# One 128-row tile for the first factors of both heads in a chunked delta-rule kernel

## The chip, the cores and the metric

The kernel runs on one core of a Trainium2 chip. The metric is the device time of one execution in microseconds (us); three runs of the kernel before took 2252.33, 2254.09 and 2258.38 us, so its median is 2254.09 us. The engines are called as the profile calls them: PE is the tensor engine's matmul and PEld its weight load, DVE the vector engine, ACT the scalar engine, POOL the GpSimd engine, SP the engine that issues most of the DMAs.

## What is computed

One layer of a hybrid decoder trunk over 1024 new tokens and 8 sequences of 8 decoded tokens, in float32. An input projection feeds three token mixers, whose gated outputs go through an output projection. The change concerns the first mixer, RWKV-7 with 16 heads of 64 features. Cut to what matters here, its reference is:

```python
def wkv7_scan(r, w, k, v, kk, a, s0):
    def step(S, inp):
        r_t, w_t, k_t, v_t, kk_t, a_t = inp
        sa = jnp.einsum('bhij,bhj->bhi', S, -kk_t)
        S = (S * w_t[:, :, None, :] + sa[..., None] * (kk_t * a_t)[:, :, None, :]
             + v_t[..., None] * k_t[:, :, None, :])
        return S, jnp.einsum('bhij,bhj->bhi', S, r_t)
```

The kernel takes 64 tokens (a chunk) at a time. Within a chunk it needs four products of every head, each a sum over the head's 64 features: the two first factors of the state's update (kk·a and k, both divided by the running decay) against the two second factors (−kk and r, both multiplied by it). Masked to the past, one of them is the triangular matrix N that is then inverted, and the others correct the outputs.

## The kernel before, in words

**Blocks and ticks.** Tokens go in two blocks (b = 0 and 1) of 512; block 0 also carries the 64 decoded tokens. In each block the input projection runs column tile after column tile as dense products on PE (`dense`, lines 237, 240, 243: three products per step, into the PSUM tile `dps`), then the output projection (lines 1360 to 1362). Between two steps of the dense products stands a call of `tick()`. Everything else is written as Python generators that issue a few instructions, then yield a number of ticks to let pass. The table `Y[b][u]` gives that number for each of the 54 yields of a unit; it is the same in both kernels. So the order of the instructions on each engine is fixed by hand when the program is built, and each engine works through its own queue in order. The dense products are the background; a side instruction on PE that waits holds up the dense products behind it.

**Units.** `rwkv_unit` (line 562) handles one pair of heads p (8 pairs) for one half u of a block: 4 chunks, or 5 in block 0's second half, where the fifth chunk holds the decoded tokens. There are 32 units, 8 of them with a fifth chunk, so 136 chunks in all. Head 0 of the pair lies in rows (partitions) 0 to 63, head 1 in rows 64 to 127. In the code `r` is the rows of the head at hand and `e` those of the other head.

**Around the change.** A unit does, in this order:
- `BE` is a chunk's first factors. It has three slots of 64 columns: slot 1 is k over the decay for both heads at once (line 647, one DVE product on 128 rows), slots 0 and 2 are the other factor of head 0 and of head 1 (line 667, written by the helper `st` on line 558, on 64 rows each). Head h takes slots h and h + 1.
- `KG` is the second factors, two heads by two slots. A head's own rows are filled by POOL (line 664, and 666 for the fifth chunk) and by DVE (line 670, through line 558). The other head's rows are written later, by `gmask_k` (line 697).
- `gmm` (line 677) makes the within-chunk products into the PSUM tiles `gp`, one matmul per chunk and head, on the 64 rows of the head. The trace counts two matmul instructions for each of these float32 products, so two chunks of both heads are 8. A unit issues its four chunks in two groups of two; a fifth chunk goes ahead as a group of its own.
- `gmask_n`, `gmask_q`, `gmask_k` read `gp` on DVE. N goes to DRAM and back for the inversion on POOL (lines 779, 780).
- `xv` is transposed into `vp` (line 732) and copied to `SV` (line 751).
- `BE` is transposed on PE, one 64-row transposition per chunk and head, into two PSUM tiles `bp` (line 758), and copied by ACT into the block-diagonal operand `Q2` (line 761).
- `bo` (line 769) sums the bonus, and so on; then the chunk recurrence runs `cp`, `W`, `cu`, `cq` (lines 871 to 895) chunk after chunk, each step a PE product, a DVE and an ACT copy.

The PSUM tiles `gp`, `vp`, `bp`, `bo`, `cq`, `fp` and others come from one pool of four buffers (`ps_s`) which they take in turn: the fifth request waits until the first is read out. Two units are under way at a time, so the recurrence of one lies between the preparations of the next on every engine.

Of the kernel before, what the change touches and what calls it, by code (L numbers as in the profile page):

```python
# [18 lines left out]
P = 128  # L19
# [35 lines left out]
def tile_trunk(  # L55
# [24 lines left out]

    # ---------------------------------------------------------------- constants
    ident = ctile([P, P], "ident")
# [24 lines left out]

    # ---------------------------------------------------------------- normalised inputs
    # the operand of a block's products, high and low parts, four feature tiles each
    act2 = [actp.tile([P, 4, 2, BLK + ND], F32R, name=f"a{j}") for j in range(4)]  # L110
# [32 lines left out]

    # ---------------------------------------------------------------- dense pieces
    wcount = [0]
# [18 lines left out]
    def out_plan(b):  # L164
        # column group, feature tile, token tiles
        if b == 1:
            return [(g, k, range(4)) for g in range(4) for k in range(NK)]
        return [(g, k, range(5)) for g in range(3) for k in range(NK)] + [(3, k, t) for t in (range(2), range(2, 5)) for k in range(NK)]
# [8 lines left out]
    class Feed:  # L177
        # the weights' pieces in their order: loads run ahead of the splits, and those ahead of the products
        def __init__(self):
# [33 lines left out]

    # generators that go on beside the products, in ticks of those
    pending, slot, seq = [], [0], [0]
# [32 lines left out]
    def dense(b, ct, hi, lo, feed, part=None):  # L248
        # part: the first half, where it is there already
        assert feed.src[feed.i] == (ct, 0)  # L250
        spans = ((0, UN), (UN, BLK + ND)) if b == 0 else ((0, BLK),)
        ps = [part or psd_tile()] + [psd_tile() for _ in spans[1:]]
        todo = list(zip(spans, ps))[1 if part else 0:]
        steps = 0
        for kh in range(4):
            piece = feed.piece(LS)
            for (t0, t1), q in todo:
                for k in range(4 * kh, 4 * kh + 4):
                    dense_k(q, hi, lo, k, piece, t0, t1, b == 1)
                    steps += 1  # L260
                    if steps < NK * len(todo):
                        tick()
                    if steps % len(todo) == 0:
                        feed.ahead(steps // len(todo) % 4)
        if b == 0:
            return [ps[0][:, :UN], ps[1][:, :UN + ND]]
        return [ps[0][:, :UN], ps[0][:, UN:]]
# [4 lines left out]
    with tc.tile_pool(name="prep", bufs=2) as pp, tc.tile_pool(name="setup", bufs=1) as sp, tc.manual_schedule():  # L272
        # the gain's row, spread over the partitions by the tensor engine
        grow = sp.tile([1, DM], F32, name="grow")
# [85 lines left out]
        def rescale(tt):  # L360
            # the scale of a tile as a diagonal, which its transposition multiplies by
            d = pp.tile([P, P], F32, name=f"dg{tt}", bufs=1)
# [175 lines left out]

    # ---------------------------------------------------------------- RWKV branch
    def shift_evac(wk, b, ct, ps, xs, u):  # L540
        # token shift of half a column tile: (1 - mu) * now + mu * before
        mu = pcol[:, MU + ct:MU + ct + 1]
# [19 lines left out]
    def rwkv_unit(wk, b, p, u, lora, lw, got, pair_ops, zk):  # L562
        # yields the steps of the dense products to let pass before it goes on
        dec = b == 0 and u == 1
# [27 lines left out]

        # decay, in-context rate, squared key norms
        sq, sqh = tmp("sq"), tmpr("sqh")
# [46 lines left out]

        BE = wk.tile([P, nch, 3, 64], F32, tag="BE", name="BE")
        yield Y[b][u][5]
        dve.tensor_mul(kp[:, :n], kp[:, :n], xk[:, :n])  # L644
        recip(0)
        yield Y[b][u][6]
        dve.tensor_mul(BE[:, :, 1, :], c3(kp), c3(Di))
        recip(1)
# [10 lines left out]
        yield Y[b][u][10]  # L659
        # phase operands of a chunk and head, in the rows of the head: keys and queries;  # L660
        # in the other head's rows: their products with the chunk's keys
        KG = wk.tile([P, nch, 2, 2, 64], F32, tag=f"KG{u}", name="KG")
        for h, r, _ in hs:
            pool_e.tensor_tensor(KG[r, 0:4, h, 1 - h, :], pair(xr)[r], Dp[r, :, 1:65], op=ALU.mult)
            if dec:
                pool_e.tensor_tensor(KG[r, 4, h, 1 - h, :].rearrange("p (b t) -> p b t", t=8), decv(xr)[r], Dd[r, :, 1:9], op=ALU.mult)
            st(BE[r, :, 2 * h, :], c3(xk)[r], dcol(HKK)[r], c3(Di)[r])
            yield Y[b][u][11]
        for h, r, _ in hs:
# [3 lines left out]
            yield Y[b][u][12]  # L673
        # within-chunk products, masked to the past
        N = wk.tile([P, nch, 64], F32, tag=f"N{u}", name="N")

        def gmm(gps, cs):
            for c in cs:
                for h, r, _ in hs:
                    pe.matmul(gps[h][:, c % 4 * P:(c % 4 + 1) * P], lhsT=BE[r, c, h:h + 2, :].rearrange("p a s -> p (a s)"),  # L680
                              rhs=KG[r, c, h].rearrange("p a s -> p (a s)"), start=True, stop=True)

# [16 lines left out]

        # X = (I - N)^-1: diagonal blocks of 16 by substitution, then blocks of 32 and 64  # L700
        ndr = drb.tile([5, 2, XS], F32, tag="ndr", name="ndr")
# [43 lines left out]
        sync.dma_start(Xu[:U], units(ndr))  # L745
        # per head: the states, then the corrections, in the rows of the head, and the values in the others
        SV = wk.tile([P, nch, 2, 64], F32, tag=f"SV{u}", name="SV")
# [6 lines left out]
        yield Y[b][u][20]  # L754
        bps = [ps_s("bp") for _ in range(2)]
        for c in range(nch):
            for h, r, _ in hs:
                pe.transpose(bps[h][:, c * 64:(c + 1) * 64], BE[r, c, h:h + 2, :].rearrange("p a s -> p (a s)"), ident[r, r])
        yield Y[b][u][21]
        for h in range(2):  # L760
            act_e.copy(Q2[:, :nch, h, h, :], c3(bps[h]))
            if not h:
                yield Y[b][u][22]
        if dec:
# [11 lines left out]
        for r in range(1, 15):  # L776
# [4 lines left out]
            if dec and r == 7:  # L781
                # states of the decoded sequences
                zp = ps_s("zp")
# [70 lines left out]
        act_e.copy(XB[64:96, :nch, 1, 32:64], d3[64:96])  # L854
        # chunk recurrence
        yc = wk.tile([P, UN + ND], F32, tag="yc", name="yc")
# [5 lines left out]

        # chunks one after the other; the decoded rows beside the first
        for c in range(4):
# [38 lines left out]
            for i, q in enumerate(cs):  # L903
                for h, _, e in hs:
                    dve.tensor_tensor(yc[e, q * 64:(q + 1) * 64], yc[e, q * 64:(q + 1) * 64], cz[i][e, h], op=ALU.add)
        # group norm (token-major), bonus and gate (feature-major)
        sm = wk.tile([P, 8], F32, tag="sm", name="sm")
# [65 lines left out]

    # ---------------------------------------------------------------- pooling branch
    NU_ = 15 + UN + NB * 23
# [32 lines left out]

    # ---------------------------------------------------------------- in-projection of a block
    def in_block(wk, b, hi, lo, feed, part, raws):  # L1010
# [28 lines left out]
        def start(ps):  # L1039
            for u in range(2):  # L1040
# [10 lines left out]
                yield 1  # L1051
            # stationary operands of both heads of a pair; the blocks between the heads stay zero
            for u in range(2):
# [65 lines left out]
        pool_group(1)  # L1119
        # spatial gating  # L1120
        vn = [wk.tile([P, 2, 512], F32, tag=f"KG{u}", name=f"vn{u}") for u in range(2)]
# [72 lines left out]
        def states():  # L1194
            # states that leave
            if b == 0:
# [47 lines left out]

    # ---------------------------------------------------------------- out-projection of a block
    def cat_load(b, k):
# [9 lines left out]
    def first_cats(b, hi, lo, raws):  # L1256
        # the first rows of the out-projection, as soon as the last column tile has read what they overwrite
        yield D[7]
# [9 lines left out]
    def out_block(op, b, hi, lo, feed, raws):  # L1268
# [12 lines left out]
        if b == 0:  # L1281
            # the decoded rows: high and low parts side by side, so that two passes carry all their products
            dk = op.tile([P, NK, 2, ND], F32R, name="dk")
# [36 lines left out]
        def next_rows(j):  # L1320
            # a quarter of the next block's normalised inputs, feature-major
            for tt in range(4):
# [41 lines left out]
        def close(g, tt, q):  # L1364
# [10 lines left out]
            if g < 3:  # L1375
# [3 lines left out]
                return  # L1379
            # the norm of a row's end  # L1380
            _, dst, rr = rows[tt]
# [27 lines left out]

        # the tiles of a group begin and end one after the other  # L1410
        lags = ((0, 0, 1, 1, 3), (0, 0, 1, 2))[b]
# [72 lines left out]
```

## Time and profile before

| what | value |
|---|---|
| median of three runs | 2254.09 us (2252.33 to 2258.38) |
| span of the profiled execution | 2252.0 us |
| within-chunk products (line 680), PE instructions | 544, of 64 rows by 128 columns, 128 moving columns |
| transpositions of `BE` (line 758), PE instructions | 272, of 64 rows by 128 columns, 64 moving columns |
| copies of `bp` into `Q2` (line 761) on ACT | 64 |
| `BE` slot 1 (line 647) on DVE | 32 |

The profile is one execution on the chip with the start and end of every instruction. The ends of matmuls are modelled, so time on PE is best read from start to start. A row of the view in order of time gives the start, the time taken, the engine, the line, the operation, what it writes and reads, for PE the rows and columns of the tile (`64*128` is 64 rows by 128 columns), the shape and the number of instructions merged; in brackets the time that the engine was idle before it and who ended that. A row of the view of waits gives who waited for whom, the sum in us, the number of times, and the longest.

### The profile page before, as it was taken

Reading aid. Unit: us, or ns where it says so; the run is one execution under the profiler, and the core shown is the slowest. Engines: PE = TensorE matmul, PEld = TensorE weight load, DVE = VectorE, ACT = ScalarE, POOL = GpSimd, SP = SyncE. Lnnn points to the kernel's source line nnn. Section 1 sums busy time; section 2 is a strip of 40 time slices with the busy share of each in tenths; the row PEclk is TensorE's granted clock in tenths of the full one; section 3 lists DMA queues with packets and bytes.
Section 4 is the critical chain, followed back from the end, with each engine's and each line's share of the span. In section 5 each row is a group of like instructions: output and inputs, shape, how many; then the busy total and the mean of one; then the engine's idle time right before and its main releaser. Section 6 shows DMA issues by size and latency. Waiting matters only on the chain. (4 is left out here: it accounts for less than half of the span.)

```text
span 2252.0 us, 40898 instructions
## 1 busy us (share of the span) xinstructions
PE 2163.5 (96%) x14706; PEld 1860.5 (83%) x14706; DVE 1212.4 (54%) x2978; ACT 1006.0 (45%) x2680; POOL 1066.7 (47%) x1820
## 2 busy tenths in 40 slices
PE   7999999999999999999999999999999999999998
PEld 6998988988889899998887777777777778887786
DVE  6477677567667523214236467767676753323313
ACT  5344554554555442223334445555556454222323
POOL 5455555554555534223335455655555463432332
PEclk9999999999999999999999999999999999999999
DMA  5232232322222233336545432222222233334634
GB/s 153 77 75 64 75 78 58 76 72 65 74 70 70 74 87 96 93 95 195 175 150 178 129 81 77 74 72 77 75 73 78 72 85 95 95 116 129 191 122 140
DMA packets 390306, 221.18 MB, mean 98 GB/s; under 512 B 124054, under 2 KB 355736, under 8 KB 389207
## 3 DMA queue, kind: packets, MB, share of 16 engines
q1 hardware_dynamic: 390104, 218.58, 34.0%
q8 instruction: 116, 1.90, 0.4%
q14 instruction: 86, 0.70, 0.1%
HBM read 191.90 MB, written 26.61 MB: 97 GB/s over the span
## 5 line engine op out<-in xcount | busy, mean ns | idle before, releaser
L237 PE MATMUL dps<-a,whi 128*128 128x256 f32 (+1 forms) x2544 | 883.6, 347 | 2.1 <-ACT whi L154 1.9
L243 PE MATMUL dps<-a,wlo 128*128 128x256 f32 (+1 forms) x2544 | 844.5, 332 | 1.1 <-POOL wlo L161 0.7
L240 PE MATMUL dps<-a,whi 128*128 128x256 f32 (+1 forms) x2544 | 843.0, 331 | 0.0
L161 POOL TENSOR_TENSOR wlo<-raw,whi 128x512 fp32r<-128x512 f32 x415 | 550.5, 1330 | 591.2 <-ACT whi L154 541.7
L237 PEld LDWEIGHTS dps<-a,whi 128*128 128x128 f32 x2544 | 484.7, 191 | 48.9 <-issue 10.2
L243 PEld LDWEIGHTS dps<-a,wlo 128*128 128x128 f32 x2544 | 484.1, 190 | 33.5 <-POOL wlo L161 1.1
L240 PEld LDWEIGHTS dps<-a,whi 128*128 128x128 f32 x2544 | 485.5, 191 | 26.0 <-issue 0.2
L154 ACT CAST whi<-raw 128x512 fp32r<-128x512 f32 x552 | 338.6, 620 | 351.9 <-PE dps L240 117.4
L161 DVE TENSOR_TENSOR wlo<-raw,whi 128x512 fp32r<-128x512 f32 x137 | 101.8, 743 | 164.3 <-ACT whi L154 163.7
L1360 PE MATMUL ops<-whi,a 128*128 128x512 f32 x448 | 176.6, 394 | 2.5 <-ACT a L1253 1.8
L1361 PE MATMUL ops<-wlo,a 128*128 128x512 f32 x448 | 176.8, 395 | 2.2 <-POOL wlo L161 1.7
L1362 PE MATMUL ops<-whi,a 128*128 128x512 f32 x448 | 175.1, 391 | 0.1
L779 POOL TENSOR_TENSOR Tu<-Xu,Nu 32x14 f32<-32x14 f32 (+9 forms) x448 | 127.0, 283 | 27.3
L780 POOL TENSOR_TENSOR Xu<-Xu,Tu 32x14 f32<-32x14 f32 (+9 forms) x448 | 120.6, 269 | 35.1
L1361 PEld LDWEIGHTS ops<-wlo,a 128*128 128x128 f32 x448 | 84.1, 188 | 23.8 <-POOL wlo L161 5.6
L1360 PEld LDWEIGHTS ops<-whi,a 128*128 128x128 f32 x448 | 84.1, 188 | 22.0 <-ACT a L1253 2.3
L898 ACT ACTIVATE ZD<-SV,DC 64x64 f32<-64x64 f32 x192 | 66.2, 345 | 79.9 <-DVE SV L558 77.2
L1362 PEld LDWEIGHTS ops<-whi,a 128*128 128x128 f32 x448 | 84.1, 188 | 19.5 <-DVE a L1254 1.8
L922 POOL TENSOR_TENSOR sv<-sv,neghalf 128x4 f32<-128x4 f32 (+1 forms) x32 | 37.1, 1158 | 132.8 <-DVE sv L921 116.5
L871 PEld LDWEIGHTS cp<-SV,KG 128*128 128x128 f32 x544 | 77.5, 190 | 24.6 <-DVE SV L558 19.8
L871 PE MATMUL cp<-SV,KG 128*128 128x64 f32 x544 | 81.4, 271 | 9.6 <-DVE SV L558 9.6
L892 PEld LDWEIGHTS cq<-SV,Q 128*128 128x128 f32 x544 | 76.4, 190 | 15.3 <-DVE SV L885 11.0
(318 smaller groups left out, 3103.2 us busy)
## 6 DMA issues: line engine op xcount, KB each, us to landing
raw<-in_w_in_dram SPq DMA_DIRECT2D x424, 256.0 KB
raw<-in_w_out_dram SPq DMA_DIRECT2D x144, 256.0 KB
raw<-cat SPq DMA_DIRECT2D x32, 256.0 KB
res<-in_x_prompt_dram SPq DMA_DIRECT2D x32, 256.0 KB
out_dram<-res SPq DMA_DIRECT2D x32, 256.0 KB
x<-in_x_prompt_dram SPq DMA_DIRECT2D x4, 1024.0 KB
x<-in_x_prompt_dram SPq DMA_DIRECT2D x6, 512.0 KB
ndr<-N SPq DMA_DIRECT2D x48, 64.0 KB
```

The lines of the kernel that those rows point to most:

```text
L154: act_e.copy(whi, raw[:, :512])
L161: eng.tensor_sub(wlo, raw[:, :512], whi.bitcast(F32))
L237: pe.matmul(o, lhsT=wh, rhs=xh, start=(k == 0), stop=False)
L240: pe.matmul(o, lhsT=wh, rhs=xl, start=False, stop=False)
L243: pe.matmul(o, lhsT=wl, rhs=xh, start=False, stop=(k == NK - 1))
L779: pool_e.tensor_tensor(tv, bc(Xu[:U, 0:r, r], 2, e), bc(Nu[:U, r, r + 1:16], 1, r), op=ALU.mult)
L780: pool_e.tensor_tensor(Xu[:U, 0:r, r + 1:16], Xu[:U, 0:r, r + 1:16], tv, op=ALU.add)
L871: pe.matmul(cw[i][:, h], lhsT=KG[:, q, h].rearrange("p a t -> p (a t)"), rhs=SV[:, q, h, :], start=True, stop=True)
L892: pe.matmul(cz[i][:, h], lhsT=Q2[:, q, h].rearrange("p a t -> p (a t)"), rhs=SV[:, q, h, :], start=True, stop=True)
L1360: pe.matmul(q, lhsT=ah, rhs=whi, start=(k == 0), stop=False)
L1361: pe.matmul(q, lhsT=ah, rhs=wlo, start=False, stop=False)
L1362: pe.matmul(q, lhsT=al, rhs=whi, start=False, stop=(k == NK - 1))
```

## The change

`BE` gets two slots in place of three: slot h holds the kk·a factor of head h in the rows of head h, and slot 1 − h the k factor in the same rows. The 128 columns of a chunk are then a single stationary operand for both heads. To fill it, the product of line 647 is made twice, on 64 rows each, since the heads' columns now differ. The second factors `KG` are set to zero in the other head's rows by two POOL memsets ahead of the products of lines 664 and 666, and `gmm` multiplies all 128 rows of `BE` by all 128 rows of `KG`; the zeros keep the heads apart. The transposition is one per chunk, of 128 rows, and fills one PSUM tile for four chunks (two in the units with a fifth chunk). One ACT copy moves both heads of up to four chunks into `Q2`.

```diff
-        BE = wk.tile([P, nch, 3, 64], F32, tag="BE", name="BE")
+        BE = wk.tile([P, nch, 2, 64], F32, tag="BE", name="BE")
...
-        dve.tensor_mul(BE[:, :, 1, :], c3(kp), c3(Di))
+        for h, r, _ in hs:
+            dve.tensor_mul(BE[r, :, 1 - h, :], c3(kp)[r], c3(Di)[r])
...
         KG = wk.tile([P, nch, 2, 2, 64], F32, tag=f"KG{u}", name="KG")
+        for h, _, e in hs:
+            pool_e.memset(KG[e, :, h], 0.0)
         for h, r, _ in hs:
...
-            st(BE[r, :, 2 * h, :], c3(xk)[r], dcol(HKK)[r], c3(Di)[r])
+            st(BE[r, :, h, :], c3(xk)[r], dcol(HKK)[r], c3(Di)[r])
...
-                for h, r, _ in hs:
-                    pe.matmul(gps[h][:, c % 4 * P:(c % 4 + 1) * P], lhsT=BE[r, c, h:h + 2, :].rearrange("p a s -> p (a s)"),
-                              rhs=KG[r, c, h].rearrange("p a s -> p (a s)"), start=True, stop=True)
+                for h in range(2):
+                    pe.matmul(gps[h][:, c % 4 * P:(c % 4 + 1) * P], lhsT=BE[:, c].rearrange("p a s -> p (a s)"),
+                              rhs=KG[:, c, h].rearrange("p a s -> p (a s)"), start=True, stop=True)
...
-        bps = [ps_s("bp") for _ in range(2)]
+        bps = [ps_s("bp") for _ in range(1 + dec)]
         for c in range(nch):
-            for h, r, _ in hs:
-                pe.transpose(bps[h][:, c * 64:(c + 1) * 64], BE[r, c, h:h + 2, :].rearrange("p a s -> p (a s)"), ident[r, r])
+            pe.transpose(bps[c // 4][:, c % 4 * P:(c % 4 + 1) * P], BE[:, c].rearrange("p a s -> p (a s)"), ident)
         yield Y[b][u][21]
-        for h in range(2):
-            act_e.copy(Q2[:, :nch, h, h, :], c3(bps[h]))
-            if not h:
-                yield Y[b][u][22]
+        for i, bp in enumerate(bps):
+            m = min(nch - 4 * i, 4)
+            act_e.copy(Q2[:, 4 * i:4 * i + m].rearrange("p c h k j -> p c (h k) j")[:, :, 0::3, :],
+                       bp[:, :m * P].rearrange("p (c h j) -> p c h j", h=2, j=64))
+        yield Y[b][u][22]
```

The lines below this are five further down in the kernel after. What moves on three engines, in the queues as the programs are built:

On DVE, a unit of block 1 before, from the first product of k to the second reciprocal (`sq` is the squared key norm, `W` the copy of the other unit's recurrence):

```order
L644 TENSOR_TENSOR kp<-kp,xk 128x256
L640 RECIPROCAL sq<-sq 128x64
L905 TENSOR_TENSOR yc<-yc,cq 64x64 x2
L875 COPY W<-cp 64x64
L647 TENSOR_TENSOR BE<-kp,Di 128x4x64
L640 RECIPROCAL sq<-sq 128x64
```

and the same place of the kernel after:

```order
L645 TENSOR_TENSOR kp<-kp,xk 128x256
L640 RECIPROCAL sq<-sq 128x64
L910 TENSOR_TENSOR yc<-yc,cq 64x64 x2
L880 COPY W<-cp 64x64
L649 TENSOR_TENSOR BE<-kp,Di 64x4x64 x2
L640 RECIPROCAL sq<-sq 128x64
```

One instruction of 128 rows has become two of 64 rows; nothing else on DVE changes its place.

On POOL, a unit of block 1 before, around the second factors (`wlo` is the low part of a piece of weights for the dense products, `kpl` a low part for `bo`):

```order
L780 TENSOR_TENSOR Xu<-Xu,Tu 32x14
L161 TENSOR_TENSOR wlo<-raw,whi 128x512 x2
L664 TENSOR_TENSOR KG<-xr,D 64x4x64 x2
L161 TENSOR_TENSOR wlo<-raw,whi 128x512
L719 TENSOR_TENSOR kpl<-kp,kph 128x256
```

and after:

```order
L785 TENSOR_TENSOR Xu<-Xu,Tu 32x14
L161 TENSOR_TENSOR wlo<-raw,whi 128x512 x2
L666 MEMSET KG 64x4x128 x2
L668 TENSOR_TENSOR KG<-xr,D 64x4x64 x2
L161 TENSOR_TENSOR wlo<-raw,whi 128x512
L723 TENSOR_TENSOR kpl<-kp,kph 128x256
```

Two memsets stand ahead of the products, behind whatever wait for the old `KG` those had.

On PE, a unit of block 1 before, around the transpositions of `BE`:

```order
L240 MATMUL dps<-a_111,whi 128x512
L243 MATMUL dps<-a_111,wlo 128x512
L758 MATMUL bp<-ident,BE 128x64 x8
L237 MATMUL dps<-a_111,whi 128x512
L240 MATMUL dps<-a_111,whi 128x512
```

and after:

```order
L240 MATMUL dps<-a_111,whi 128x512
L243 MATMUL dps<-a_111,wlo 128x512
L762 MATMUL bp<-ident,BE 128x128 x4
L237 MATMUL dps<-a_111,whi 128x512
L240 MATMUL dps<-a_111,whi 128x512
```

Eight transpositions of 64 rows are four of 128 rows, at the same place. The within-chunk products keep their number and their places.

## The prediction

> **What bounds the kernel now.** I read the page first, then the chain that ended last, then the waits, and then PE and DVE in order of time at the places of the change.
>
> ```profile
> span 2252.0 us, 40898 instructions
> ...
> PE 2163.5 (96%) x14706; PEld 1860.5 (83%) x14706; DVE 1212.4 (54%) x2978; ACT 1006.0 (45%) x2680; POOL 1066.7 (47%) x1820
> ...
> PE dps L243 6%; PE dps L237 6%; PE dps L240 6%; PE ops L1362 2%; PE ops L1361 2%; PE ops L1360 2%; DVE sq L640 1%; DMA raw<-in_w_out_dram 1%; DVE KG L558 1%; PE gp L680 1%; PE cq L892 1%; DVE BE L558 1%; DVE kp L558 1%; DVE kp L644 1%; DVE SV L558 1%
> ```
>
> PE is busy nearly throughout and DVE half of the time. Yet the last line, the chain by line, has DVE's preparation of `kp`, `sq`, `BE` and `KG` in it. The chain in order of time shows how it gets there (start, time, what), here in a unit of block 1:
>
> ```profile
> 1380.01 0.41 PE cq L892 x4
> 1380.44 0.28 DVE SV L558
> ...
> 1382.57 0.83 DVE BE L647
> ...
> 1389.40 0.48 DVE KG L558
> 1390.05 1.27 DVE KG L558
> 1391.45 0.68 PE gp L680 x6
> ```
>
> From 1380.4 to 1391.3 the chain stays on DVE: a queue without a gap, released by PE's `cq`, until the within-chunk products can go on. The waits confirm it, and hold two more rows that the change touches:
>
> ```profile
> PE gp L680 <- DVE KG L558: 13.8, 18, 3.0
> PE bp L758 <- ACT SV L751: 1.9, 7, 0.3
> PE bo L769 <- ACT yf L963: 1.2, 7, 0.2
> ```
>
> So at `gp` PE waits for DVE, and what makes DVE later there makes PE later by as much.
>
> **The change, PE's own work.** First the rows: a group of eight products behind no wait (block 1, a unit's second group), eight products of 128 rows of the same length (line 1181), eight transpositions of 64 rows and four of 128 rows (line 1128), each with the dense products around.
>
> ```profile
> 1393.30 0.40 PE L243 MATMUL dps<-a,wlo 128*128 128x512 f32 x1
> 1393.63 0.71 PE L680 MATMUL gp<-KG,BE 64*128 64x128 f32 x8
> 1394.27 0.50 PE L237 MATMUL dps<-a,whi 128*128 128x512 f32 x1
> ```
>
> ```profile
> 1994.70 0.39 PE L243 MATMUL dps<-a,wlo 128*128 128x512 f32 x1
> 1994.93 1.05 PE L1181 MATMUL mixp<-wsT,vn 128*128 128x128 f32 x8
> 1995.74 0.48 PE L237 MATMUL dps<-a,whi 128*128 128x512 f32 x1
> ```
>
> ```profile
> 1438.42 0.39 PE L243 MATMUL dps<-a,wlo 128*128 128x512 f32 x1
> 1438.74 0.46 PE L758 MATMUL bp<-ident,BE 64*128 64x64 f32 x8
> 1439.13 0.50 PE L237 MATMUL dps<-a,whi 128*128 128x512 f32 x1
> ```
>
> ```profile
> 1901.21 0.39 PE L243 MATMUL dps<-a,wlo 128*128 128x512 f32 x1
> 1901.44 0.60 PE L1128 MATMUL tp<-ident,vf 128*128 128x128 f32 x4
> 1901.80 0.47 PE L237 MATMUL dps<-a,whi 128*128 128x512 f32 x1
> ```
>
> *Products.* From dense start to dense start the 64-row group takes 1394.27 − 1393.30 = 0.97 us, the 128-row group 1.04. "All rows" therefore gains nothing: the two heads already share the array, and what 64-row tiles lose on the way in (the first starts 0.33 behind the dense product, where the 128-row one starts 0.23 behind) they win back by running beside each other. There are 40 such groups behind no wait (8 in block 0's first halves, 16 in its decoded halves, 16 in block 1): 40 × 0.07 = 2.8 us more, and I take 3.5, since eight stand directly behind other 64-row products and paid only one of the two switches.
>
> The Trainium skill's page TensorEngine Tiling (Array Packing), sections Key Properties and Theoretical Speedup, says that tiles run in parallel, up to twofold for two row tiles, and that a change of tiling mode drains the engine. By the twofold alone each group would take 0.74 more, 40 × 0.74 = 30 us, an estimate that the two groups above contradict (0.07).
>
> *First groups.* Here the second head's products wait for DVE:
>
> ```profile
> 1428.38 0.48 PE L680 MATMUL gp<-KG,BE 64*128 64x128 f32 x2
> 1429.37 0.68 PE L680 MATMUL gp<-KG,BE 64*128 64x128 f32 x6 [0.51 <-DVE KG L558]
> 1429.98 0.50 PE L240 MATMUL dps<-a,whi 128*128 128x512 f32 x1
> ```
>
> After the wait six instructions take 0.61 to the next dense product; six of 128 rows take 6/8 of 1.04 − 0.23, which is 0.61. Nothing won, nothing lost. The first head's still go ahead, as their operands are complete earlier. For the eight groups of a decoded chunk (four instructions) I have no such pair of rows; a little is saved on the switch, between 0 and 2 us, and I take −1.
>
> *Transpositions.* Alone: 0.71 against 0.59, 0.12 less. In 25 of 32 units it is that or less (beside other small tiles the switch was shared); I take 0.08: −2.0 us. In seven units of block 0 one more thing stands in the way, the second `bp` buffer, which waits for `vp` to be copied away:
>
> ```profile
> 178.49 0.44 PE L955 MATMUL fp<-ident,yc 128*128 128x128 f32 x2
> 178.85 0.27 PE L758 MATMUL bp<-ident,BE 64*128 64x64 f32 x1
> 179.40 0.46 PE L758 MATMUL bp<-ident,BE 64*128 64x64 f32 x7 [0.28 <-ACT SV L751]
> 179.79 0.42 PE L237 MATMUL dps<-a,whi 128*128 128x320 f32 x1
> ```
>
> `fp` and `bp` take 1.30 us. With one buffer and 128 rows it would be six transpositions in a row, at 0.36 for four: 0.54. That is 0.76 × 7 = −5.3 us. One request fewer also lets `bo` take an older buffer: its wait above, −1.2. The copies on ACT become fewer and larger; `Q2` is read many ticks later by `cq`, so nothing waits for them.
>
> PE's own sum: 3.5 + 0 − 1.0 − 2.0 − 5.3 − 1.2 = −6.0 us.
>
> **The change, POOL.** Two memsets a unit, behind the wait for the old `KG`.
>
> ```profile
> L1064 POOL MEMSET Q<- 64x256 f32 x6 | 1.8, 306 | 0.3
> ```
>
> ```profile
> 1425.67 1.60 POOL L664 TENSOR_TENSOR KG<-xr,D 64x256 f32<-64x256 f32 x2 [2.28 <-PE cp L871]
> ```
>
> Twice the elements, so at most 0.61 each and 1.2 a unit, 39 us in all on an engine that is half idle. They push the products of `KG` from 1427.27 to about 1428.5, which is still ahead of DVE's `KG`, for which `gp` waited until 1429.37. I take 0 for the path; the cover is that 0.9 us. Behind them stands the next `wlo`, 1.2 us later, whose piece is used three pieces on.
>
> **The change, DVE.** One product more in each of the 32 units, in the queue of the chain above.
>
> ```profile
> L647 DVE TENSOR_TENSOR BE<-kp,Di 128x256 f32<-128x256 f32 x24 | 19.1, 795 | 0.0
> ```
>
> ```profile
> 1420.49 0.41 DVE L647 TENSOR_TENSOR BE<-kp,Di 128x256 f32<-128x256 f32 x1
> ```
>
> The length depends on the columns, so each half costs what the whole did. It takes 0.41 alone, as here, 0.83 in the chain above, and 0.795 on average. The difference is POOL: with a `wlo` under way DVE's product ends after it. The second half comes just behind the first, when that turn is over, so 0.41 is nearer than 0.795 for itself. But it can also push a later product of DVE into POOL's turn, as in the decoded halves:
>
> ```profile
> 286.80 0.47 DVE L647 TENSOR_TENSOR BE<-kp,Di 128x320 f32<-128x320 f32 x1
> ...
> 287.66 0.42 DVE L558 SCALAR_TENSOR_TENSOR Di<-tha,Di 128x320 f32<-128x320 f32 x1
> ...
> 288.46 0.50 DVE L558 SCALAR_TENSOR_TENSOR SV<-cq,DC,ZD 64x64 f32<-64x64 f32 x2
> ```
>
> ```profile
> 287.84 1.38 POOL L161 TENSOR_TENSOR wlo<-raw,whi 128x512 fp32r<-128x512 f32 x1 [1.85 <-ACT whi L154]
> ```
>
> `Di` starts 0.18 ahead of `wlo` now. With 0.47 more in front it starts 0.29 behind it, and ends after 289.2 instead of at 288.08; `SV`, which PE's `cp` needs, follows. That is over 1.1 us for a 0.47 us product. I take 1.2 for the 8 decoded halves and 0.41 for the other 24: 9.6 + 9.8 = 19.4 us. The bounds: 0, where a later product waits for POOL's turn anyway and swallows the delay, and 32 × 0.795 = 25.4, or 1.2 in every unit, 38.
>
> The Trainium skill's page SBUF — State Buffer, section Who interferes with whom, says that a DVE instruction with two SBUF inputs contends with a GpSimd instruction that reads SBUF, and not with one that only writes; 0.41 against 0.83 above agrees with the first half. By the second half the memsets take no turn from DVE; no run here shows that yet.
>
> **Sum.** 2252.0 − 6.0 + 19.4 = 2265.4 us of span. The median of the runs is 2.1 above the profiled span, so 2267.5 us, 0.6% slower. A measurement of this kernel can tell about 0.3% from no change, 6.8 us: faster is below 2247.3, slower above 2260.9.
>
> **The rivals.**
> *Swallowed (20%).* DVE's delay disappears in turns that POOL holds anyway, and PE keeps its 6.0 us: 2248, and a little less where PE's shorter waits shorten others. The point from which it decides is 6.0 / 32 = 0.19 us of delay a unit: below it the change is a gain. For it: the 0.83 in the chain is such a turn. Against: the chain runs without a gap for 11 us, and most of its instructions never wait for POOL. Half of this case lies under 2247.3.
> *The bare price (25%).* 0.41 or 0.47 in every unit and no turns: 24 × 0.41 + 8 × 0.47 = 13.6, so 2261.7, on the border; half of it counts as no change.
> *The clock (15%).* Longer waits of PE cost clock:
>
> ```profile
> 299.00:303.00 4.00, 4.00 (x22) 3.24 (x20) 3.78 (x17) 2.00 (x6) 0.36 (x1) 0.57 0.00 0
> ```
>
> In this stretch, behind a wait for DVE in a decoded half, the granted clock (third figure from the end) is 0.57: 4.0 × 0.43 = 1.7 us lost. If the eight first halves of block 0 catch it too, 8 × 1.7 = 13.6 more: 2281.
>
> My forecast has the remaining 40%. Faster 0.10, the same 0.10 + 0.12 = 0.22, slower 0.68. The range 2247 to 2285 takes in most of the clock case and half of the swallowed one; the rest, under 2 in 10, lies outside on both sides.
>
> **What would show it.** Right: the second `BE` product 0.41 long and directly behind the first; `Di` in the decoded halves ending after POOL's `wlo`; `gp` waiting longer for `KG` in first groups; second groups 1.04 us from dense to dense; no wait of `bp` for `SV`, nor of `bo` for `yf`. Wrong: first groups no later than now (the delay was swallowed), memsets over 0.9 us a pair longer than taken, so that POOL's `KG` is what `gp` waits for, or groups of 128 rows that start closer than 0.1 us apart.

## The result and the profile after

The kernel after takes 2269.49 us (median of six runs, 2265.53 to 2271.35 and one disturbed run of 2912.75 that stands apart and is in no ratio; without it the median is 2268.92); the kernel before beside it 2254.23 us (six runs). The ratio is 1.0058, with a 95% interval of 1.0039 to 1.0077: slower by 0.6%, where 2267.5 was predicted. The profiled execution has a span of 2267.2 us, 15.2 more than before.

The page of the kernel after, its span and its engines:

```profile
span 2267.2 us, 40719 instructions
...
PE 2156.0 (95%) x14570; PEld 1883.0 (83%) x14570; DVE 1228.4 (54%) x3010; ACT 1003.1 (44%) x2656; POOL 1103.0 (49%) x1884
```

PE is busy for 7.5 us less than before and yet ends later: it waits more. DVE is busy for 16.0 us more, POOL (the memsets) for 36.3. Where PE waits is in the view of waits (who for whom, sum in us, times, longest). The kernel before:

```profile
PE cp L871 <- DVE SV L558: 9.6, 20, 0.8
PE d L823 <- DVE Q L836: 8.9, 7, 1.4
...
PE cq L892 <- DVE SV L885: 4.5, 9, 0.6
```

and the kernel after:

```profile
PE cp L876 <- DVE SV L558: 18.7, 21, 1.2
PE gp L684 <- DVE KG L558: 13.0, 25, 2.5
PE d L828 <- DVE Q L841: 11.2, 7, 1.7
PE cq L897 <- DVE SV L890: 10.5, 9, 1.4
...
PE cp L876 <- ACT SV L863: 5.4, 7, 0.8
```

The recurrence (`cp`, `cq`) waits 9.1 and 6.0 us longer for the state that DVE writes, `d` 2.3 longer, and `cp` has a new wait of 5.4 for ACT. The wait at `gp`, of which the prediction expected the loss, went from 13.8 to 13.0. The waits of `bp` (1.9) and `bo` (1.2) are gone. The sum is +18.9 us, of the 22.7 by which PE idles longer (15.2 of span and 7.5 less of work).

How the two 64-row products make `cp` late is seen in a decoded half (the same place that the prediction showed at 286.80). DVE and POOL, and then PE, in order of time, in the kernel after:

```profile
294.10 0.97 DVE L649 TENSOR_TENSOR BE<-kp,Di 64x320 f32<-64x320 f32 x2
295.10 0.55 DVE L640 RECIPROCAL sq<-sq 128x64 f32<-128x64 f32 x1
295.57 1.20 DVE L558 SCALAR_TENSOR_TENSOR Di<-tha,Di 128x320 f32<-128x320 f32 x1
296.70 0.54 DVE L640 RECIPROCAL sq<-sq 128x64 f32<-128x64 f32 x1
297.16 0.50 DVE L558 SCALAR_TENSOR_TENSOR SV<-cq,DC,ZD 64x64 f32<-64x64 f32 x2
```

```profile
295.14 1.28 POOL L161 TENSOR_TENSOR wlo<-raw,whi 128x512 fp32r<-128x512 f32 x1 [1.85 <-ACT whi L154]
```

```profile
297.39 0.76 PE L876 MATMUL cp<-SV,KG 128*128 128x64 f32 x4 [1.20 <-DVE SV L558]
```

The two products take 0.97 where the one took 0.47. `Di` now starts 0.43 behind `wlo` instead of 0.18 ahead of it, and takes 1.20 instead of 0.42: it ends 0.35 behind the end of `wlo`. From the start of the product to the start of `SV` it is 3.06 us where it was 1.66, and `cp` waits 1.20. In the kernel before it did not wait here:

```profile
288.73 0.72 PE L871 MATMUL cp<-SV,KG 128*128 128x64 f32 x4
```

### The profile page after: what moved, and what is told of

Its sections match the earlier page's. It is cut to its first block, busy times and chain, and to the rows that moved or that the text cites. A ratio compares the mean times of both kernels' runs of the same rounds, so it can differ in the third digit from the quotient of the medians.

```text
span 2267.2 us, 40719 instructions
## 1 busy us (share of the span) xinstructions
PE 2156.0 (95%) x14570; PEld 1883.0 (83%) x14570; DVE 1228.4 (54%) x3010; ACT 1003.1 (44%) x2656; POOL 1103.0 (49%) x1884
## 5 line engine op out<-in xcount | busy, mean ns | idle before, releaser
L684 PE MATMUL gp<-KG,BE 128*128 128x128 f32 x544 | 86.0, 294 | 15.9 <-DVE KG L558 13.0
```

The source lines that it names most:

```text
L684: pe.matmul(gps[h][:, c % 4 * P:(c % 4 + 1) * P], lhsT=BE[:, c].rearrange("p a s -> p (a s)"), rhs=KG[:, c, h].rearrange("p a s -> p (a s) ...
```

## Experiments

Every kernel ran in five rounds beside the kernel before (medians of that 2253.2 to 2254.5). The theory D: the loss is the second product of DVE, with the turns of POOL that it runs into. The rivals: A, the 128-row products on PE cost it, since the heads no longer share the array; M, the memsets on POOL cost it. A summary, then each in turn. A half-clock cell is a stretch of 3.41 us in which PE's granted clock is 0.5; the table has their number in the profiled execution, the mean granted clock of the runs in the ratio, and an estimate of the difference to the kernel before at equal clock. The last section works it out.

```
                        median us   ratio    95% interval       half-clock  granted  at equal
                                                                cells       clock    clock, us
before (81 runs)        2253.4                                  11          0.9900
after                   2269.5      1.0058   1.0039 to 1.0077   11          0.9910   +16.7
split only              2278.2      1.0112   1.0090 to 1.0133   17          0.9865   +20.0
split, decoded halves   2261.9      1.0036   1.0022 to 1.0051   12          0.9901    +9.6
split, other halves     2267.5      1.0052   1.0036 to 1.0069   16          0.9882    +9.8
memsets only            2260.4      1.0039   1.0021 to 1.0056   21          0.9853    +1.1
after, 64-row products  2272.8      1.0081   1.0062 to 1.0101   11          0.9892   +17.3
after, one product      2248.3      0.9977   0.9962 to 0.9992    6          0.9936    +0.5
  and 64-row products   2254.9      0.9998   0.9982 to 1.0014   16          0.9885    -2.1
after, zeros by ACT     2276.2      1.0097   1.0073 to 1.0121   10          0.9903   +23.4
uniform                 2242.2      0.9947   0.9933 to 0.9962    4          0.9958    -2.3
uniform, 64 rows        2246.7      0.9968   0.9954 to 0.9982   11          0.9907    -6.1
uniform, zeros by ACT   2248.8      0.9978   0.9964 to 0.9993    4          0.9955    +3.6
before, filled wait     2254.0      1.0005   0.9993 to 1.0018    9          0.9910    +2.2
```

**The split alone, in the kernel before.**

```diff
-        dve.tensor_mul(BE[:, :, 1, :], c3(kp), c3(Di))
+        for h, r, _ in hs:
+            dve.tensor_mul(BE[r, :, 1, :], c3(kp)[r], c3(Di)[r])
```

> The kernel before with one edit: the k product of a unit is written as two 64-row instructions of DVE (tile of three slots, products and transpositions on 64 rows as before, no memsets). Theory D (the change costs what its extra DVE instruction costs, the lateness of DVE's queue paid by PE at the recurrence and the factors): the DVE term alone, without PE's gain of about 6, so 2254 + 19 = 2273 us (2268 to 2278); at the bare length of the two instructions 2254 + 14 = 2268. Theory A (the 128-row products and the lost packing cost it): 2254 (2251 to 2257). Theory M (the memsets on POOL cost it, through POOL's half of KG): 2254 (2251 to 2257).

2278.2 us, 1.0112: one added DVE instruction a unit costs 25 us, more than the whole change and just above the range of D. Its waits:

```profile
PE cp L872 <- DVE SV L558: 18.8, 21, 1.4
PE gp L681 <- DVE KG L558: 14.9, 15, 4.0
PE cq L893 <- DVE SV L886: 14.3, 16, 1.4
```

+9.2 at `cp` and +9.8 at `cq`, 19.0 in all; `gp` +1.1. A and M expected nothing here. The granted clock was 0.9865 against 0.9900; at equal clock the split costs 20.0.

**The split in the decoded halves alone, and in the others alone.** The same two lines, under `if dec` and under `if not dec`.

> The kernel before with the k product in two 64-row instructions in the eight decoded halves alone (320 columns). Theory D with POOL's turns: in each, the second instruction (0.5) brings the step on Di behind POOL's wlo (Di 1.20 in place of 0.42), so SV and with it cp come 1.2 to 1.4 later; eight of these are +10 to +11, so 2254 + 10 = 2264 us (2260 to 2268). Theory B (only the instruction's own length counts): 8 x 0.45 = 3.6, so 2257.

> The kernel before with the k product in two 64-row instructions in the 24 halves without decoded rows alone (256 columns). Theory D: 24 x 0.41 to 0.45 = +10, so 2264 us (2259 to 2270); the price of the split in all halves was 25, so the two kernels' prices should make up about that. Theory B: the same 10. If the lateness is swallowed in these halves (rival): 2254 to 2257.

2261.9 and 2267.5 us: +7.5 and +13.0 against the 2254.45 beside them, or 1.0036 and 1.0052. The waits tell the two terms apart. Decoded halves alone:

```profile
PE cp L872 <- DVE SV L558: 17.8, 27, 1.2
...
PE cq L893 <- DVE SV L886: 4.5, 9, 0.6
```

and the other halves alone:

```profile
PE cq L893 <- DVE SV L886: 14.3, 16, 1.4
PE cp L872 <- DVE SV L558: 10.6, 14, 1.4
```

The eight decoded halves pay at `cp` (9.6 to 17.8: 8.2, or 1.0 each), the 24 others at `cq` (4.5 to 14.3: 9.8, or 0.41 each) and hardly at `cp` (1.0). Theory B, by the bare length, had 3.6 for the decoded halves. In medians the two make 20.5, less than the 25 of all halves together; at equal clock 9.6 and 9.8 make up the 20.0.

**One product again, in the kernel after.**

```diff
-        for h, r, _ in hs:
-            dve.tensor_mul(BE[r, :, 1 - h, :], c3(kp)[r], c3(Di)[r])
+        dve.tensor_mul(BE[:, :, 1, :], c3(kp), c3(Di))
...
         recip(2)
+        act_e.copy(BE[rs[1], :, 0, :], BE[rs[1], :, 1, :])
```

> The changed kernel with the k product as one 128-row instruction of DVE again, into slot 1 of both heads, and ACT copying head 1's half to slot 0 (64 rows, 256 or 320 elements) one step later; 128-row products, memsets and transposition stay. Theory D: the DVE term goes and PE's gain stays, 2254 - 6 = 2248 (2245 to 2253), a little more if ACT's copy is waited for. Theory A: 2267 to 2271, unchanged. Theory M: 2267 to 2271, unchanged.

2248.3 us, 0.9977 [0.9962, 0.9992], as D expected: with all else of the change in place, the loss is gone and 4.9 us are won. Its runs had a granted clock of 0.9936 against 0.9900; at equal clock nothing is won (+0.5). Its waits, of all that stand for DVE:

```profile
PE gp L684 <- DVE KG L558: 14.2, 24, 2.2
PE d L828 <- DVE Q L841: 11.9, 8, 1.7
PE cp L876 <- DVE SV L558: 9.3, 20, 0.6
...
PE cq L897 <- DVE SV L890: 0.7, 2, 0.4
```

`cp` is back at 9.3. Between this kernel and the kernel after lie 21 us, or 16 at equal clock, for 32 instructions of DVE, with 32 copies by ACT in their place.

**The products back on 64 rows, without the memsets, in the kernel after and in the one above.**

```diff
-        for h, _, e in hs:
-            pool_e.memset(KG[e, :, h], 0.0)
...
-                for h in range(2):
-                    pe.matmul(gps[h][:, c % 4 * P:(c % 4 + 1) * P], lhsT=BE[:, c].rearrange("p a s -> p (a s)"),
-                              rhs=KG[:, c, h].rearrange("p a s -> p (a s)"), start=True, stop=True)
+                for h, r, _ in hs:
+                    pe.matmul(gps[h][:, c % 4 * P:(c % 4 + 1) * P], lhsT=BE[r, c].rearrange("p a s -> p (a s)"),
+                              rhs=KG[r, c, h].rearrange("p a s -> p (a s)"), start=True, stop=True)
```

> The changed kernel with its within-chunk products back on 64 rows (each head's own rows of the two-slot tile), without the memsets; the split product and the one 128-row transposition of a chunk stay. Theory D: the loss stays, less the 3.5 us that the 128-row products cost behind no wait: 2266 (2262 to 2270). Theory A: 2250 (2246 to 2254), since the products give everything back and the transposition still gains. Theory M: 2248 to 2254, since the memsets are gone.

> The changed kernel with both edits undone that the runs before undid one at a time: the k product one 128-row instruction with ACT's copy of head 1's half, and the within-chunk products on 64 rows without the memsets; only the two-slot tile and the one 128-row transposition of a chunk are left of the change. If the two edits add up: 2248 + 3 = 2251 us (2247 to 2255). If the 128-row products are dearer on a path on which DVE is not late (theory A): 2242 to 2246.

2272.8 and 2254.9 us, so 0.0023 and 0.0021 of the ratio more than with 128 rows and memsets. A and M fall: undoing what they blame makes the kernel slower, by 3 to 7 us. At equal clock it is 0.6 slower and 2.6 faster, and neither is near the loss of 15. D's own expectation (3.5 less) missed as well. The four corners add up: the split is worth 0.0081 to 0.0083, products with memsets −0.0021 to −0.0023, whatever the other is. What is left in the last kernel, one transposition a chunk, is worth nothing that can be measured in the ratio (0.9998), and 2.1 at equal clock, with ACT's extra copy in it.

**The memsets alone, in the kernel before.**

```diff
+        for h, _, e in hs:
+            pool_e.memset(KG[e, :, h], 0.0)
```

> The kernel before with one edit: POOL zeroes the other head's rows of KG in two memsets ahead of its two products, nothing reads the zeros. Theory D: POOL's 1.2 us lie under the cover of 0.9 us and DVE's two later products, so 2254 to 2257. Theory M: the loss of the change, 15 us or with PE's gain added back 21 us, so 2269 to 2275. Theory A: 2254.

2260.4 us, 1.0039: between the theories, and with a wide spread (2253.6 to 2270.9). The waits for DVE:

```profile
PE d L825 <- DVE Q L838: 11.8, 8, 1.7
PE cp L873 <- DVE SV L558: 9.3, 20, 0.6
...
PE cq L894 <- DVE SV L887: 0.7, 2, 0.4
```

The memsets make `d` wait 2.9 longer and `cq` 3.8 shorter; the lengths do not carry the 7 us. Its profiled execution has ten half-clock cells more than that of before, and its twelve runs had the lowest granted clock of all, 0.9853: at equal clock +1.1 is left, as D had it.

**The zeros written by ACT, in the kernel after and in the uniform kernel.**

```diff
-        for h, _, e in hs:
-            pool_e.memset(KG[e, :, h], 0.0)
...
             yield Y[b][u][11]
+            if not h:
+                for g, _, e in hs:
+                    act_e.copy(KG[e, :, g].rearrange("p c a t -> p c (a t)"), bc(zero[e], 1, nch))
```

> The changed kernel with the two memsets of KG taken from POOL: ACT copies the zeros, one step later; all else of the change stays. Theory M: 2254 or below. Theory D: the split product still sets the lateness; POOL's memsets are worth 0 (2269) to 5 us (2264) where POOL's KG ends last in block 1.

> The uniform kernel with the other head's rows of KG zeroed by ACT, in two copies from a tile of zeros one step later, in place of POOL's two memsets. In block 1 the first product began as POOL's KG ended, so if POOL's 1.04 us there are on the path: some 0.2 to 0.5 us in 14 halves, 3 to 7 us, so 2237 (2234 to 2241). If DVE's KG ends no earlier and is the next late by the same: 2242, unchanged. If ACT's two copies (1.2 us, in order with its casts) are waited for instead: 2244 to 2250.

2276.2 and 2248.8 us, each about 6.6 slower than with POOL's memsets (1.0097 against 1.0058, 0.9978 against 0.9947), and about as much at equal clock (6.7 and 5.9). M falls again, and so does my hope that POOL's 1.04 us in block 1 were on the path: the memsets are better placed on POOL than on ACT.

**One order of the factors for both heads.** Slot 0 holds the kk·a factor of both heads, slot 1 the k factor, so that each is one 128-row instruction.

```diff
-        for h, r, _ in hs:
-            dve.tensor_mul(BE[r, :, 1 - h, :], c3(kp)[r], c3(Di)[r])
+        dve.tensor_mul(BE[:, :, 1, :], c3(kp), c3(Di))
...
-            st(BE[r, :, h, :], c3(xk)[r], dcol(HKK)[r], c3(Di)[r])
+            if not h:
+                st(BE[:, :, 0, :], c3(xk), dcol(HKK), c3(Di))
...
+            act_e.copy(Q2[:, 4 * i:4 * i + m, 0, 0, :], bv_[:, :, 0, :])
+            for o in range(2):
+                act_e.copy(Q2[rs[o], 4 * i:4 * i + m, 1, 1, :], bv_[rs[1 - o], :, 1, :])
```

> The changed kernel with one order of the factors for both heads (decay-rate factor in slot 0, key factor in slot 1), so that each of the two is written by one 128-row instruction of DVE: two instructions less than the changed kernel, one less than the kernel before. The masks of head 1 read the other rows of the products, and ACT moves head 1's transposed halves in two 64-row copies (three copies in place of one). Theory D: DVE's second product of rank one goes as well, 24 x 0.37 = 9 and some 0.5 in each decoded half below 2248, so 2236 (2230 to 2246). Theories A and M: 2267 to 2271.

> The uniform kernel (both factors by one 128-row instruction each) with its within-chunk products back on 64 rows and without the memsets. In the two pairs of kernels that differ in this alone the 128-row products with the memsets were the faster by 3 to 7 us (ratios 1.0081 against 1.0058, 0.9998 against 0.9977). If that is their own price on PE or the clock: 2242 + 5 = 2247 us (2243 to 2251). If it hung on DVE's lateness (now less): 2242 or below.

2242.2 us, 0.9947 [0.9933, 0.9962], the fastest of all: 12 us under before and 27 under after. With 64-row products 2246.7, where 2247 was expected. D's 2236 was too much for the first: DVE's instruction fewer is there (1193.3 us of busy time, 19 less than before), but `gp`'s wait rose to 17.4 and the new wait of `cp` for ACT to 8.4. At equal clock only 2.3 of the 12 us are left: most of the gain is the clock, 0.9958. The traces show where it comes from. The wait of `d` for `Q`, behind which five of the eight stretches of half clock in the kernel before stand, is short here, and none stands behind it:

```profile
PE d L830 <- DVE Q L843: 4.2, 6, 0.7
```

**A wait of PE filled.**

```diff
             qv = q[:, :nch * 32].rearrange("p (c t) -> p c t", t=32)
+            if dec and nm == "d2":
+                for _ in range(4):
+                    pe.matmul(q, lhsT=hi[0][:, 0, 0:P], rhs=hi[0][:, 0, 0:512], start=True, stop=True)
```

> The kernel before with four products of 128 rows by 512 columns put into PE's wait for Q in the eight decoded halves (in front of d's own products, into the same PSUM tile, which d's products then overwrite; they add nothing to the result). In the traces a stretch of half clock, one or two cells of 3.41 us, follows PE idles of over 1.2 us, and seven such cells of the kernel before stand behind this wait of 1.44. Theory of the clock: the idle falls to about 0.5, these cells go, and with about 1.2 us for each the kernel is some 8 us faster, 2246 (2242 to 2249), with a smaller spread of its runs. If the cells come from the wait's lateness and not from PE's idling: no change, 2254; if the four products (0.9 us) delay d: 2254 to 2258.

2254.0 us, 1.0005. The experiment missed its place: the long wait stands in the halves without decoded rows, while DVE prepares a decoded half, and my four products stood in the decoded halves' own `d`.

```profile
301.72 0.66 PE L826 MATMUL d<-Q,X 64*64 64x32 f32 x16 [1.44 <-DVE Q L839]
```

The wait is as long as before. Nothing follows for the clock; 32 more products of 128 by 512 cost under 0.2%.

## Why the prediction was right

**The extra DVE product, +19.4.** Right in size and in both parts. The split raised the waits at `cp` and `cq` by 19.0 us, 8.2 from the decoded halves (predicted 9.6, by `Di` slipping behind `wlo`: 1.0 to 1.2 each) and 9.8 from the others (predicted 24 × 0.41 = 9.8). In medians it is dearer, 25 us on the kernel before and 18 to 21 on the change, but the clock is in these: at equal clock it is 20.0, of it 9.6 in the decoded halves and 9.8 in the others. So neither the swallowed case nor the bare price came about.

**Where it is paid.** Wrong. The prediction said that "at `gp` PE waits for DVE, and what makes DVE later there makes PE later by as much", and so `gp` was to wait longer in first groups; its wait went from 13.8 to 13.0. The preparation of a unit and the recurrence of the unit ahead share DVE's queue, and PE reaches `cp` and `cq` first: it pays there, and by the time of `gp` both are late by the same. The chain on which the prediction saw no gap also held `SV`; that was the row to follow.

**PE's own sum, −6.0.** Too large. That the experiment with one product gives −4.9 is luck: at equal clock that kernel wins nothing (+0.5), and in the change without its split 16.7 − 20.0 = −3.3 is left. The total came out near 2267.5 because the large term was right and this one small. Of the terms:

*Groups behind no wait* take 1.04 us from dense to dense, as read off line 1181 (kernel after, 1408.46 − 1407.42):

```profile
1407.42 0.39 PE L243 MATMUL dps<-a,wlo 128*128 128x512 f32 x1
1407.65 1.05 PE L684 MATMUL gp<-KG,BE 128*128 128x128 f32 x8
1408.46 0.48 PE L237 MATMUL dps<-a,whi 128*128 128x512 f32 x1
```

So the twofold of the Trainium skill's page TensorEngine Tiling (Array Packing), section Theoretical Speedup, does not show in this place: undoing the packing cost 0.07 us a group and not the 0.74 worked out from it.

*Products with memsets together* were put at +2.5 and 0, and came out at −5 in the ratios of each of three pairs of kernels. By the estimate of the last section that is the clock, for which the sum had no term: with 128 rows and memsets it was 0.9910, 0.9936 and 0.9958, with 64 rows 0.9892, 0.9885 and 0.9907. Why is not shown, and the memsets alone went the other way. At equal clock the pairs give −0.6, +2.6 and +3.8, so the +2.5 is about right in two of them, and so is the 0 for the memsets (+1.1 alone). But the memsets do not leave the waits as they were. In the pair of rows that follows, DVE is held up beside POOL's product and not beside the memset. In the kernel with the split alone, DVE's `lora` beside POOL's product:

```profile
297.76 0.58 DVE L1021 TENSOR_TENSOR lora<-lraw,lora 128x256 fp32r<-128x256 f32 x1
```

```profile
297.37 0.69 POOL L665 TENSOR_TENSOR KG<-xr,D 64x256 f32<-64x256 f32 x1 [1.80 <-PE cp L872]
```

and in the kernel after, beside the memset:

```profile
298.62 0.36 DVE L1025 TENSOR_TENSOR lora<-lraw,lora 128x256 fp32r<-128x256 f32 x1
```

```profile
298.27 1.31 POOL L666 MEMSET KG<- 64x640 f32 x2 [1.84 <-PE cp L876]
```

0.58 against 0.36. The second half of the rule in the Trainium skill's page SBUF — State Buffer, section Who interferes with whom (a GpSimd instruction that only writes takes no turn from DVE), agrees with this pair. POOL's products move by the length of the memsets, beside other instructions of DVE, and the waits shift, in the kernel with the memsets alone by −3.8 at `cq` and +2.9 at `d`, together −0.9. The memset itself took 0.52 (64 × 512), under the bound of 0.61, and 0.63 in the decoded halves (64 × 640).

*Transpositions alone* are 0.58 (1452.32 to 1452.90), predicted 0.59. *The seven places in block 0*, −5.3, and `bo`, −1.2: `fp` and `bp` do take 0.63 now instead of 1.30, and both waits are gone. But the gain is given back 5 us later:

```profile
183.11 0.44 PE L960 MATMUL fp<-ident,yc 128*128 128x128 f32 x2
183.38 0.60 PE L762 MATMUL bp<-ident,BE 128*128 128x128 f32 x4
183.74 0.39 PE L237 MATMUL dps<-a,whi 128*128 128x320 f32 x1
...
188.80 1.15 PE L876 MATMUL cp<-SV,KG 128*128 128x64 f32 x8 [0.78 <-ACT SV L863]
```

ACT runs without a gap from the copy of `vp` (at 179.09 before, 183.71 after) to that `SV`. Before, and after:

```profile
182.33 0.38 ACT L761 COPY Q<-bp 128x256 f32<-128x256 f32 x1
182.73 0.62 ACT L154 CAST whi<-raw 128x512 fp32r<-128x512 f32 x1
183.38 0.28 ACT L854 COPY XB<-d 32x160 f32<-32x160 f32 x1
183.67 0.51 ACT L858 COPY SV<-Zc 64x64 f32<-64x64 f32 x2
184.21 0.35 ACT L860 ACTIVATE ZD<-Zc,DC 128x64 f32<-128x64 f32 x1
184.57 0.37 ACT L761 COPY Q<-bp 128x256 f32<-128x256 f32 x1
```

```profile
186.96 0.59 ACT L766 COPY Q<-bp 128x512 f32<-128x512 f32 x1
187.57 0.62 ACT L154 CAST whi<-raw 128x512 fp32r<-128x512 f32 x1
188.21 0.28 ACT L859 COPY XB<-d 32x160 f32<-32x160 f32 x1
188.51 0.51 ACT L863 COPY SV<-Zc 64x64 f32<-64x64 f32 x2
```

The prediction said of ACT's copies that nothing waits for them. Nothing reads them early, but `SV` stands behind them in ACT's queue: one copy of 0.59 ahead of it in place of 0.38, with the second 0.37 behind it. Before, `cp` started without a wait:

```profile
184.38 1.00 PE L871 MATMUL cp<-SV,KG 128*128 128x64 f32 x8
```

From `fp` to `cp` it was 184.38 − 178.49 = 5.89 before and is 5.69 now: 0.2 won, where 0.76 and 0.17 were booked. Seven places make 1.4, not 6.5. That nothing waits behind ACT's copies is the step of the sum that failed, and the kernel that has only the transposition left of the change agrees: −2.1 at equal clock, with ACT's extra copy in it, where −2.0 and −6.5 were booked.

**The clock, 15%.** The profiled executions of before and after have 11 half-clock cells each, and the runs a granted clock of 0.9900 and 0.9910, so the difference holds none of it. The change's eight first halves did not all catch a cell, as this rival had it, and a cell costs 1.1 us, not 1.7 (last section).

## What to carry to other kernels

Count the instructions of an engine that is half idle as if it were full wherever its queue holds, between two of them, what the bound engine waits for next; and look for that wait in the *other* stage that shares the queue, not in the stage being edited. One 128-row instruction of DVE in place of two of 64 rows was worth more here (16 us at equal clock) than the choice of the array's rows (under 4 either way). Where runs scatter with the granted clock, compare kernels at equal clock before a term of a few us is called right. A wait that goes is only won as far as the next queue allows: follow the time from its place to the next instruction of the bound engine that reads something else.

## What was not expected: the half-clock cells

In the traces PE's granted clock is 1.0 or 0.5, and the stretches of 0.5 within one execution, but for its very start and end, begin on one grid of 3.41 us and last one, two or three such cells. Two equal waits in the kernel after, with the mean granted clock of the stretch behind them (third figure from the end):

```profile
481.96 0.66 PE L828 MATMUL d<-Q,X 64*64 64x32 f32 x16 [1.67 <-DVE Q L841]
...
569.45 0.87 PE L828 MATMUL d<-Q,X 64*64 64x32 f32 x16 [1.67 <-DVE Q L841]
```

```profile
482.00:486.00 4.00, 3.55 (x36) 3.17 (x37) 3.86 (x14) 0.75 (x3) 0.63 (x1) 1.00 0.16 49
569.40:573.20 3.80, 3.75 (x30) 3.69 (x31) 3.67 (x13) 0.63 (x3) 0.72 (x1) 0.55 0.20 57
```

After the first the clock stays; after the second it is halved. I summed PE's idle time by cells of the grid, over the fourteen traces of this case from 70 us on, and counted how often the next cell ran at half clock:

```
PE idle in a cell, us   cells   next one at half clock
under 1.0               8538    26
1.0 to 1.2               176    10
1.2 to 1.4                55    15
1.4 to 2.0                89    60
over 2.0                  46    46
```

So a wait of 1.4 to 1.7 us mostly halves the clock if it falls into one cell (60 of 89), and mostly doesn't if the grid cuts it in two. In block 0 the waits for `Q` come every 85.5 us in the kernel with one product, close to 25 cells (85.33): there the first three are cut and the clock stays, and behind each of the next three it is halved. Which it is can differ from one execution to the next: the runs of this kernel have clocks from 0.991 to 0.996. The Trainium skill's page TensorE: Matmul & The Clock Gate, Part 1, has a free-running window of this length, which agrees; the advice of that page's section Why this matters for your kernels, to keep idle gaps under some 3 us, is too mild for these traces, where 2 us within a cell always sufficed.

A cell's price can be read in the kernel with one product, where the wait for `Q` comes once a pair: `d` starts at 210.7, 296.2, 381.7, 467.2, 553.8 and 640.1, that is 85.5, 85.5, 85.5 and, with one cell each behind the fourth and the fifth, 86.6 and 86.3: 0.8 to 1.1 us.

The runs give the same price, since each has its mean granted clock on record, and this counts the cells: 0.996 with 4 in the profiled execution, 0.990 or 0.991 with 11, 0.983 with 21. The 81 runs of the kernel before, beside the experiments, reach from 2245.5 us at 0.995 to 2261.9 at 0.987; a straight line through them falls by 1.5 us for 0.001 of the clock, and one cell (1.7 of 2252 us lost) is 0.00076 of it, so 1.1 us. The last column of the summary is the mean of a kernel's runs less that of these 81 (2253.4), with 1.5 us added for each 0.001 by which its clock lies above 0.9900. It is an estimate: in the kernels with twelve runs the line falls by 1.1 to 2.4, so a difference of 0.005 in the clock leaves it open by some 3 us. The split's two parts and the change's 16.7 stand on clocks at most 0.0018 from that of the kernel before, so they are better known, to about 1 us.

What draws the clock of one kernel above that of another is seen for the uniform kernel alone (its short waits of `d`). Why 128-row products with memsets had the higher clock in all three pairs, while memsets alone had the lowest of all, stays open, and the experiment on the cause of the cells missed its place.
